# Seven block products for eight in half of a down projection, woven with the up projection, on one core

## Chip, cores, metric

The kernel runs on one core of a Trainium2 chip. The metric is the device time of one execution in microseconds (us), the median of three runs. The profile is one further execution of the same program with the hardware profiler on.

## The reference, cut to what matters

One decoder layer over 256 tokens (and 16 meta tokens) with `D_MODEL = 2048`, all float32. Two gated mixers come first; the change concerns what follows them:

```python
    h = h + rms_norm(m @ w_o[l], g_post_mix[l])
    u = rms_norm(h, g_pre_mlp[l])
    f = jnp.square(jax.nn.relu(u @ w_up[l])) @ w_down[l]     # w_up 2048 x 8192, w_down 8192 x 2048
    h = h + rms_norm(f, g_post_mlp[l])
return h[:, N_META:]
```

## The kernel before

**Split products.** Every float32 operand is kept as two parts, a high part `hi` (a rounding copy, ScalarE, line 176) and the rest `lo` (`raw - hi`, VectorE, line 179). A product is three TensorE products: hi x hi, hi x lo, lo x hi. Weights come from HBM in blocks of 1 MB (a `raw` tile, 128 x 2048 float32), loaded by the SP queue (line 173), split by `high` and `low` in `open_chunk`, and used once. There are three raw tiles and three hi/lo pairs, taken in turn, so the split of block n+2 can start only when the matmuls of block n-1 have ended. `fetch(ahead=2)` does this while block n is being used.

**The MLP** goes in `NP = 4` pieces of 2048 hidden features. In each piece the up projection comes first: `project` (called with `mm2`, lines 342 and 348) makes 128 features x 256 tokens per accumulator, weights standing in the array and tokens moving, 16 blocks of 1 MB. `evac_up` adds the two halves of an accumulator (`halves`), applies relu and square, and splits the result into `f_act`. Then the down projection: `project_t` with `block_t` (line 593) multiplies 128 tokens of `f_act` (standing) with 512 columns of `w_down` (moving); each 1 MB block takes 24 matmuls, 12 for each half of the tokens. `evac_down` adds each finished block to `F`, the sum over the four pieces. The scale of the second norm (`r2`) is applied at the end, in `times_g`.

**Order.** Each engine runs its instructions in the order in which the program issues them (`tc.manual_schedule()`); this order is written out by hand. Small work is put between matmuls by `drain` from a list `pending`.

**Ending.** The last 512 output columns are done with the second half of the tokens in two strips of 256 columns (`last_half`), so that the norm and the store of the first half run beside the last matmuls. `finish_down` multiplies by the norm factor, adds the residual and stores.

Of the kernel before, what the change touches and what calls it, by code (L numbers as in the profile page):

```python
# [11 lines left out]
ALU = mybir.AluOpType  # L12
# [4 lines left out]
CW = 512  # L17
RMS_EPS = 1e-6
LN_EPS = 1e-5


@with_exitstack
def hybrid_block(ctx: ExitStack, tc: tile.TileContext, ins: dict, out: bass.AP):
# [83 lines left out]
    NP = FF // D  # L107
    G0 = PW + 2 * CC
    HALF = (2 * CK, CW // 2)
    HALF_CW = CW // 2  # L110
# [229 lines left out]
    def mm2_high(acc, hi, act, k, cs, start, ts=slice(0, T), stop=False):  # L340
        off = act.shape[3] - T
        nc.tensor.matmul(acc.rearrange("p (a t) -> p a t", a=2)[:, :, ts], hi[:, k[0], cs],  # L342
                         act[:, k[1], :, off + ts.start:off + ts.stop], start=start, stop=stop,
                         skip_group_check=True)
# [31 lines left out]
    def halves(acc, name):  # L376

        t = tmp.tile([P, T], F32, tag="v", bufs=5, name=f"half_{name}")
        nc.scalar.copy(t, acc[:, :T])
        s = tmp.tile([P, T], F32, tag="v", bufs=5, name=f"sum_{name}")  # L380
        nc.vector.tensor_add(s, t, acc[:, T:])
        return s

    def split(dst, k, src):
        def f():
            nc.scalar.copy(dst[:, k, 0, :], src)
            nc.vector.tensor_sub(dst[:, k, 1, :], src, f32(dst[:, k, 0, :]))
        late.append(f)
# [415 lines left out]

    for n in range(NB - 1):
        project_t(m_of, KD, evac_o(n), f"o{n}")
        if n == 0:
            g_mlp = big.tile([P, D], F32, tag="c", name="g_mlp")
            nc.gpsimd.dma_start(g_mlp, ins["g_post_mlp"].broadcast_to([P, D]))
    u2 = m  # L810

    def u2_tiles(t0, n, k0, nk):
# [17 lines left out]
                f32(u2[:, k0 + i, 0, sl]), op0=ALU.mult, op1=ALU.subtract)  # L830
        return high, low


    f_act = []

    def f_of(k):
        return f_act[k // (KD // 2)][:, k % (KD // 2), :, :]

    def evac_up(j0):
        def f(j, acc):  # L840
            s = halves(acc, f"up_{j0 + j}")
            nc.vector.scalar_tensor_tensor(s, s, 0.0, s, op0=ALU.max, op1=ALU.mult)
            split(f_act[(j0 + j) // (KD // 2)], (j0 + j) % (KD // 2), s)
        return f

# [86 lines left out]
    up_high(2, 1)  # L932
    up_low(2)
    hi, lo = fetch()
    for b in range(2):
        room = big.tile([P, b * LINE + KD * T], F32R, tag=f"s{b}", name=f"f_act{b}")
        f_act.append(room[:, b * LINE:].rearrange("p (k a t) -> p k a t", k=KD // 2, a=2))
    for j, acc in enumerate(accs):
        for k in range(CK):
            kk = 3 * CK + k  # L940
            cs = slice(j * P, (j + 1) * P)
            if kk < KD - 1:
                mm2(acc, hi, lo, u2, (k, kk), cs, False, False)
            else:
                mm2_low(acc, lo, u2, (k, kk), cs)
                mm2_high(acc, hi, u2, (k, kk), cs, False, stop=True)
        flush(1)
        evac_up(0)(j, acc)
    ssq2 = const.tile([P, NT, NB], F32, name="ssq2")


    r2 = const.tile([P, NT], F32, name="r2")

    def square_h1(t, n):
        def f():
            square_of(h1[:, t, block(n)], ssq2, t, n)
        return f

    def scale2():
        nc.vector.reduce_sum(r2, ssq2, axis=mybir.AxisListType.X)  # L960
        nc.vector.tensor_scalar(r2, r2, 1.0 / D, RMS_EPS, op0=ALU.mult, op1=ALU.add)
        nc.vector.reciprocal(r2, r2)

    pending += [(1, square_h1(t, n)) for t in range(NT) for n in range(NB)]
    pending += [LATER, LATER, (1, scale2)]

    F = big.tile([P, NT, D], F32, tag="k8", bufs=2, name="F")
    ov = out[0].rearrange("(t p) d -> p t d", p=P)

    def evac_down(i, n):  # L970
        sl = block(n)

        def f(t, acc):
            if i == 0:
                nc.vector.tensor_copy(F[:, t, sl], acc)
                return
            nc.vector.tensor_add(F[:, t, sl], F[:, t, sl], acc)
            if i == NP - 1:
                square_of(F[:, t, sl], norm3.ssq, t, n, scale=r2[:, t:t + 1])
                times_g(t, sl)  # L980
                if n == NB - 2:
                    norm3.start(t)
        return f

    def times_g(t, sl):
        nc.vector.scalar_tensor_tensor(F[:, t, sl], F[:, t, sl], r2[:, t:t + 1], g_mlp[:, sl],
                                       op0=ALU.mult, op1=ALU.mult)

    def finish_down(t, cuts):

        for n, (c0, c1) in enumerate(zip(cuts, cuts[1:])):
            sl = slice(c0, c1)
            nc.vector.scalar_tensor_tensor(F[:, t, sl], F[:, t, sl], norm3.r[:, t], h1[:, t, sl],
                                           op0=ALU.mult, op1=ALU.add)
            (nc.sync, nc.scalar)[n % 2].dma_start(ov[:, t, sl], F[:, t, sl])
# [10 lines left out]
    last_f = acc_tiles("f_last", NT + 1)  # L1006
    last_ssq = const.tile([P, 2], F32, name="last_ssq")
    col_halves = [slice(h * HALF_CW, (h + 1) * HALF_CW) for h in range(2)]

    def last_half(h, kc, hi, lo):  # L1010
        cs = col_halves[h]
        block_t(last_f[1 + h][:, cs], hi[:, :, cs], lo[:, :, cs], f_of, kc, KD, 1)

    n = KD // CK - 3
    for kc in range(n):
        hi, lo = fetch()
        block_t(last_f[0], hi, lo, f_of, kc, KD, 0)
        for h in range(2):
            last_half(h, kc, hi, lo)
    three = [fetch(2 - i) for i in range(3)]  # L1020
    for i, (hi, lo) in enumerate(three):
        block_t(last_f[0], hi, lo, f_of, n + i, KD, 0)
    sl = block(NB - 1)
    nc.vector.tensor_add(F[:, 0, sl], F[:, 0, sl], last_f[0])
    square_of(F[:, 0, sl], norm3.ssq, 0, NB - 1, scale=r2[:, 0:1])
    norm3.finish(0)
    times_g(0, sl)
    finish_down(0, range(0, D + 1, CW))
    for h, cs in enumerate(col_halves):
        for i, (hi, lo) in enumerate(three):  # L1030
            last_half(h, n + i, hi, lo)
        sl = slice((NB - 1) * CW + cs.start, (NB - 1) * CW + cs.stop)
        s = tmp.tile([P, HALF_CW], F32, tag="v", bufs=5, name=f"last_{h}")
        nc.vector.tensor_add(s, F[:, 1, sl], last_f[1 + h][:, cs])
        junk = tmp.tile([P, CW], F32, tag="junk", bufs=1, name=f"sq_last_{h}")
        nc.scalar.activation(junk[:, cs], s, AF.Square, scale=r2[:, 1:2],
                             accum_out=last_ssq[:, h:h + 1])
        nc.vector.scalar_tensor_tensor(F[:, 1, sl], s, r2[:, 1:2], g_mlp[:, sl],
                                       op0=ALU.mult, op1=ALU.mult)
        if h == 0:  # L1040
            nc.vector.scalar_tensor_tensor(norm3.v[:, 1], last_ssq[:, 0:1], 1.0 / D,
                                           norm3.v[:, 1], op0=ALU.mult, op1=ALU.add)
    for f in norm3.steps(1, last_ssq[:, 1:2]):
        f()
    finish_down(1, (0, HALF_CW, CW + HALF_CW, 2 * CW + HALF_CW, D - HALF_CW, D))


# [23 lines left out]
```

## Time and profile before

| what | value |
|---|---|
| median of 3 runs | 1234.48 us (1234.24 to 1234.86) |
| the profiled execution: its own time / span of its instructions | 1235.01 us / 1233.1 us |
| TensorE busy, granted clock | 1222.1 us (99%), 0.998 |
| VectorE busy / ScalarE busy | 807.6 us (65%) / 541.6 us (44%) |
| HBM read | 234.12 MB, 192 GB/s over the span |

The page gives busy time by engine and by group of instructions; "idle before" is the time in which an engine waited just before that group, and what ended it. Because matmuls are pipelined, a matmul of 512 columns shows a duration of 389 ns while the next one starts 227 ns after it; rates are therefore read from chains of many matmuls.

### The profile page before, as it was taken

Reading aid. Unit: us, or ns where it says so; the run is one execution under the profiler, and the core shown is the slowest. Engines: PE = TensorE matmul, PEld = TensorE weight load, DVE = VectorE, ACT = ScalarE, POOL = GpSimd, SP = SyncE. Lnnn points to the kernel's source line nnn. Section 1 sums busy time; section 2 is a strip of 40 time slices with the busy share of each in tenths; the row PEclk is TensorE's granted clock in tenths of the full one; section 3 lists DMA queues with packets and bytes.
Section 4 is the critical chain, followed back from the end, with each engine's and each line's share of the span. In section 5 each row is a group of like instructions: output and inputs, shape, how many; then the busy total and the mean of one; then the engine's idle time right before and its main releaser. Section 6 shows DMA issues by size and latency. Waiting matters only on the chain.

```text
span 1233.1 us, 15685 instructions
## 1 busy us (share of the span) xinstructions
PE 1222.1 (99%) x6572; PEld 1059.6 (86%) x6572; DVE 807.6 (65%) x938; ACT 541.6 (44%) x571; POOL 6.1 (0%) x18
## 2 busy tenths in 40 slices
PE   9999999999999999999999999999999999999997
PEld 8999988888888888898888888888888888888886
DVE  5799978999676654685654456554475544556555
ACT  6633344443574443564533345433344433445432
POOL 1000000000000000000000000000000000000000
PEclk9999999999999999999999999999999999999999
DMA  8655555655548565645656656556656556566551
GB/s 258 212 187 172 171 190 187 204 188 190 195 149 316 191 212 198 204 150 193 196 181 203 190 189 201 191 187 203 190 185 205 189 187 203 179 201 202 190 186 69
DMA packets 130757, 237.22 MB, mean 192 GB/s; under 512 B 3985, under 2 KB 29905, under 8 KB 130160
## 3 DMA queue, kind: packets, MB, share of 16 engines
q1 hardware_dynamic: 128768, 229.78, 57.0%
q0 software_dynamic: 768, 4.35, 0.9%
q10 hardware_dynamic: 1152, 2.11, 0.5%
q8 instruction: 51, 0.84, 0.3%
q14 instruction: 18, 0.15, 0.0%
HBM read 234.12 MB, written 2.10 MB: 192 GB/s over the span
## 4 chain that ended last, share of the span: by engine, by line
PE 98%; DMA 1%; DVE 1%; ACT 0%; ACTq 0%; DVEq 0%; issue 0%
PE acc_dn L593 26%; PE acc_up L342 19%; PE acc_gate L593 14%; PE acc_up L348 10%; PE acc_o L593 5%; PE acc_v L337 4%; PE acc_g L337 4%; PE acc_z L337 4%; PE acc_co L593 4%; PE acc_po L593 4%; PE acc_f_last L593 2%; PE acc_o_last L593 2%; DMA x_in<-in_x_dram 1%; PE ht L818 0%; PE mt L713 0%; PE xt L284 0%
## 5 line engine op out<-in xcount | busy, mean ns | idle before, releaser
L179 DVE TENSOR_TENSOR lo<-raw,hi 128x2048 fp32r<-128x2048 f32 (+1 forms) x236 | 495.2, 2101 | 352.3 <-ACT hi L176 351.9
L176 ACT CAST hi<-raw 128x2048 fp32r<-128x2048 f32 (+1 forms) x236 | 413.7, 1757 | 556.1 <-PE acc_dn L593 190.6
L342 PE MATMUL acc_up<-m,hi 128*128 128x512 f32 (+1 forms) x1008 | 338.0, 387 | 0.0
L593 PE MATMUL acc_dn<-hi,f_act 128*128 128x512 f32 x960 | 296.4, 389 | 0.0
L348 PE MATMUL acc_up<-m,lo 128*128 128x256 f32 x992 | 272.2, 278 | 0.0
L342 PEld LDWEIGHTS acc_up<-m,hi 128*128 128x128 f32 x1008 | 186.8, 188 | 38.3
L593 PEld LDWEIGHTS acc_dn<-hi,f_act 128*128 128x128 f32 x960 | 180.2, 188 | 37.5
L593 PE MATMUL acc_dn<-lo,f_act 128*128 128x512 f32 x480 | 186.9, 389 | 0.0
L348 PEld LDWEIGHTS acc_up<-m,lo 128*128 128x128 f32 x992 | 185.7, 188 | 0.5
L593 PE MATMUL acc_gate<-hi,u 128*128 128x512 f32 x512 | 158.6, 390 | 0.0
L403 DVE SCALAR_TENSOR_TENSOR c<-a,taps,c 128x256 f32<-128x256 f32 x240 | 115.5, 484 | 6.6
L593 PEld LDWEIGHTS acc_gate<-hi,u 128*128 128x128 f32 x512 | 96.1, 188 | 20.0
L593 PEld LDWEIGHTS acc_dn<-lo,f_act 128*128 128x128 f32 x480 | 90.1, 188 | 18.5
L593 PE MATMUL acc_gate<-lo,u 128*128 128x512 f32 x256 | 99.6, 389 | 0.0
L593 PE MATMUL acc_o<-hi,m 128*128 128x512 f32 x192 | 59.6, 390 | 0.0
L593 PEld LDWEIGHTS acc_gate<-lo,u 128*128 128x128 f32 x256 | 48.1, 188 | 9.8
L337 PE MATMUL acc_v<-u,hi 128*128 128x272 f32 x256 | 49.8, 293 | 0.0
L337 PE MATMUL acc_g<-u,hi 128*128 128x272 f32 x256 | 47.5, 287 | 0.0
L337 PE MATMUL acc_z<-u,hi 128*128 128x272 f32 x256 | 47.4, 287 | 0.0
L593 PEld LDWEIGHTS acc_o<-hi,m 128*128 128x128 f32 x192 | 36.0, 188 | 7.4
L593 PE MATMUL acc_co<-hi,s_act 128*128 128x512 f32 x128 | 40.4, 392 | 0.0
L337 PEld LDWEIGHTS acc_v<-u,hi 128*128 128x128 f32 x256 | 39.8, 188 | 0.4
(222 smaller groups left out, 1061.5 us busy)
## 6 DMA issues: line engine op xcount, KB each, us to landing
raw<-in_w_up_dram SPq DMA_DIRECT2D x64, 1024.0 KB, 5.3
raw<-in_w_down_dram SPq DMA_DIRECT2D x64, 1024.0 KB, 5.1
raw<-in_w_in_dram SPq DMA_DIRECT2D x54, 1024.0 KB, 5.0
raw<-in_w_o_dram SPq DMA_DIRECT2D x16, 1024.0 KB, 5.0
raw<-in_w_pool_out_dram SPq DMA_DIRECT2D x8, 1024.0 KB, 5.2
raw<-in_w_conv_out_dram SPq DMA_DIRECT2D x8, 1024.0 KB, 5.1
raw<-in_w_in_dram SPq DMA_DIRECT2D x8, 256.0 KB, 8.0
h<-in_x_dram POOLq DMA_DIRECT2D x1, 2048.0 KB, 9.6
```

The source lines that it names most:

```text
L176: nc.scalar.copy(hi[:, sl, :], raw[:, sl, :])
L179: nc.vector.tensor_sub(lo[:, sl, :], raw[:, sl, :], f32(hi[:, sl, :]))
L337: nc.tensor.matmul(acc, w[:, k[0], cs], act[:, k[1], a, off:], start=first and n == 0, stop=last and n == 2)
L342: nc.tensor.matmul(acc.rearrange("p (a t) -> p a t", a=2)[:, :, ts], hi[:, k[0], cs], act[:, k[1], :, off + ts.start:off + ts.stop], start ...
L348: nc.tensor.matmul(acc[:, :T], lo[:, k[0], cs], act[:, k[1], 0, off:], start=False, stop=stop, skip_group_check=True)
L403: nc.vector.scalar_tensor_tensor(c, conv["a"][:, q, i:i + T], taps[:, q, i:i + 1], c, op0=ALU.mult, op1=ALU.add)
L593: nc.tensor.matmul(acc, act(kk)[:, a_, ts_], w_[:, k, :], start=kk == 0 and n == 0, stop=kk == nk - 1 and n == 2)
```

## The change

The MLP goes in eight pieces of 1024 hidden features. In each piece the down projection sees the weights as two rows (512 features each, index 1 and 2) of four column blocks of 512. Column blocks 2 and 3 are multiplied as before (products `X1` to `X4`, 24 matmuls each), but accumulate over all pieces in four PSUM banks. Column blocks 0 and 1 form a 2 x 2 block matrix B11, B12, B21, B22; with the two halves of the tokens as the other side this is a 2 x 2 by 2 x 2 block product, done in Strassen's manner (Winograd's form) as seven products `P1` to `P7` of 12 matmuls each in place of eight. For these, sums of weight blocks are made in place in the raw tile (four per piece, `SUM_FOR`), four sums and differences of the activations (`S1` to `S4`) are made and split, and each of the seven results is added from its bank to `F` (`give`).

The order of products is a written text, up products `U..` between the others (`U0b1` is the up block for feature half 0, pair b, half 1 of the inner dimension; `+` means the next piece). Everything in this part is put into a `Plan` with an engine, a cost, reads and writes; `Plan.order` is a list scheduler that keeps the given order on TensorE and SP and chooses the order on VectorE and ScalarE. Up blocks are 1024 x 256 instead of 512 x 512 (still 1 MB). The raw tiles are five (three as before, two in the place of tiles no longer needed). The factor of the second norm is now needed before the squares: `R` is two small matmuls that spread it over the partitions, and relu multiplies by it. `g_mlp` is loaded at the end on the SP queue and not early on the POOL queue. The ending keeps the two strips for the last two products.

```diff
+class Plan:
+    HOP = 0.15
+    FIXED = ("PE", "SP")
+    def add(self, engine, cost, f, reads=(), writes=(), late=0.0):
...
+    def order(self):
...
-    for i in range(NP):
-        standing_chunks.update(range(len(stream), len(stream) + NB * KD // CK))
-        for h in range(NB):
-            stream += columns(w_up, 0, KD, i * D + h * CW)
-        for n in range(NB):
-            stream += columns(w_down, i * KD, KD, n * CW)
+    PF = 2 * CW
+    NP = FF // PF
...
+    FIRST_PIECE = "U1a0 U1a1 R U1b0 U1b1 P1 X1 X3"
+    PIECE = "U1a0 U1a1 P1 X1 U1b0 U1b1 X3"
+    NEXT = "U0a0+ P5 X2 P6 X4 P7 U0a1+ P3 U0b0+ P2 U0b1+ P4"
+    LAST_PIECE = "U1a0 P1 U1a1 U1b0 U1b1 X1 P5 X2 P6 P3 P7 P2 P4 X3 X4"
...
+    SUM_FOR = {"P5": ("B11", "B12"), "P6": ("B11", "B22"), "P7": ("B12", "B22"),
+               "P4": ("B11", "B21")}
...
+            if what == "sum":
+                a_, b_ = (room_of[r][:, :CK * CW] for r in rooms)
+                plan.add("DVE", 2.29, lambda: nc.vector.tensor_add(a_, a_, b_),
+                         reads=names, writes=names[:1])
...
+                plan.add("ACT", 1.91, high, reads=names, writes=(f"hi{q}",))
+                plan.add("DVE", 2.29, low, reads=names + [f"hi{q}"], writes=(f"lo{q}",))
...
+        def relu():
+            s = box["s"]
+            nc.vector.scalar_tensor_tensor(s, s, 0.0, rb[:, None, :T].broadcast_to([P, 2, T]),
+                                           op0=ALU.max, op1=ALU.mult)
...
+    BANK = {"P1": "a", "P6": "a", "P7": "a", "P4": "a", "P5": "b", "P3": "b", "P2": "b"}
...
+    def product_block(m_, s, i):
+        h, f = FORM[s]
+        plan.add("PE", 2.72, lambda: down(banks[BANK[s]], split_at[m_], h, f, s in OPENS, True),
+                 reads=half_names(m_) + act_names(h, f), writes=(BANK[s],))
+        give(s, i)
...
+        if s == "R":
+            plan.add("PE", 0.9, rows2, reads=("diag2",), writes=("b",))
...
-    for i in range(NP):
-        for h in range(1 if i == 0 else 0, NB):
-            project(u2, KD, evac_up(h * CW // P), f"up{i}{h}", shape=(CK, CW), fill=1.0)
-        for n in range(NB):
-            if i < NP - 1 or n < NB - 1:
-                project_t(f_of, KD, evac_down(i, n), f"dn{i}{n}")
...
+    finish_down(1, (0, 384, D // 2, D // 2 + CW, D - HALF_CW, D))
+    plan.emit()
```

More of the change, by code (lines that the diff above doesn't have):

```diff
@@ L934, in hybrid_block @@
     hi, lo = fetch()
-    for b in range(2):
[L936 to L943, printed above, removed]
-            else:
[L945 to L948, printed above, removed]
+    flush()
@@ new lines, in raw_of @@
+    def raw_of(s, i):
+        return (RAW_OF.get(s, s), i)
+    uses = []
+    for m_, (s, i) in enumerate(products):
+        if m_ >= len(opened):
+            if s in SUM_FOR:
+                uses.append((m_, "sum", [(r, i) for r in SUM_FOR[s]]))
+            uses.append((m_, "split", [raw_of(s, i)]))
+    last_use = {}
+    to_load = []
+    for n, (_, _, raws_) in enumerate(uses):
+        for r in raws_:
+            if r not in last_use:
+                to_load.append(r)
+            last_use[r] = n
@@ new lines, in hybrid_block, with load, loads @@
+    free_rooms = list(room_of)
+    room_at = {}
+    def load(r):
+        src, (rows, width) = source(*r)
+        room = room_at[r] = free_rooms.pop(0)
+        plan.add("SP", 3.2, lambda: nc.sync.dma_start(
+            room_of[room].rearrange("p (k c) -> p k c", k=rows), src),
+            writes=(f"raw{room}",), late=2.0)
+    def loads():
+        while to_load and free_rooms:
+            load(to_load.pop(0))
+    split_at = {}
+    first_n = at["n"] - len(opened)
+    for m_, (hi_, lo_, _) in enumerate(opened):
+        split_at[m_] = {"hi": hi_, "lo": lo_}
@@ L965, in hybrid_block @@
[L965 to L983, printed above, removed]
@@ new lines, in hybrid_block @@
+    loads()
+    for t in range(NT):
+        for n in range(NB):
+            plan.add("ACT", 0.92, square_h1(t, n), writes=("junk", "ssq2"))
+    plan.add("DVE", 0.4, mean2, reads=("ssq2",), writes=("v2",))
+    plan.add("ACT", 0.3, root2, reads=("v2",), writes=("q2",))
+    plan.add("DVE", 1.2, diag2, reads=("q2", "v2"), writes=("diag2",))
+    unscaled = [(0, pr, 0, accs[2 * pr:2 * pr + 2], [f"x{pr}{j}" for j in range(2)])
+                for pr in range(2)]
+    m_ = 0
+    tail = len(products) - 2
@@ new lines, in sum_of_squares, with times_g @@
+    def sum_of_squares(t, n):
+        src, name = tokens_of(t, n)
+        plan.add("ACT", 0.92, lambda: square_of(src, norm3.ssq, t, n), reads=(name,),
+                 writes=("junk", f"ssq{t}{n}"))
+    def times_g(t, n):
+        src, name = tokens_of(t, n)
+        plan.add("DVE", 0.69, lambda: nc.vector.tensor_mul(
+            dst_of(t, n * CW, (n + 1) * CW), src, g_mlp[:, block(n)]),
+            reads=(name, f"raw{room_g}"), writes=(f"out{t}{n}", name if n < 2 else f"raw{room_f}"))
+    for t in range(NT):
+        for n in range(NB - 1):
+            sum_of_squares(t, n)
+            times_g(t, n)
+        plan.add("DVE", 0.4, lambda t=t: norm3.start(t),
+                 reads=[f"ssq{t}{n}" for n in range(NB - 1)], writes=(f"v{t}",))
@@ L989, in finish_down @@
+    plan.add("DVE", 0.69, lambda: nc.vector.tensor_copy(Fx[:, 1, 1, :], banks["x11"]),
+             reads=("x11",), writes=("rest", f"raw{room_f}"))
     def finish_down(t, cuts):
         for n, (c0, c1) in enumerate(zip(cuts, cuts[1:])):
[L992 to L995, printed above, removed]
@@ L1027, in hybrid_block @@
[L1027 to L1042, printed above, removed]
@@ new lines, in hybrid_block @@
+    ends = [(m_, "X3"), (m_ + 1, "X4")]
+    for w, s in ends:
+        h = AT[s][0]
+        plan.add("PE", 2.72, lambda w=w, h=h: down(banks["x10"], split_at[w], h, A1, False, h == 1),
+                 reads=half_names(w) + act_names(h, A1), writes=("x10",))
+    sum_of_squares(0, NB - 1)
+    times_g(0, NB - 1)
+    plan.add("DVE", 1.5, lambda: norm3.finish(0), reads=("v0", f"ssq0{NB - 1}"), writes=("r0",))
+    finish_down(0, range(0, D + 1, CW))
+    col_halves = [slice(h * HALF_CW, (h + 1) * HALF_CW) for h in range(2)]
```

378 lines of the change are left out of this document (335 added, 43 removed).

## Prediction

> **What bounds the kernel now.** I read the page first, then the chain of waits in order of time, the table by windows, the groups with shapes kept apart, and stretches of the timeline. Page: busy time, and the chain by engine.
>
> ```profile
> PE 1222.1 (99%) x6572; PEld 1059.6 (86%) x6572; DVE 807.6 (65%) x938; ACT 541.6 (44%) x571; POOL 6.1 (0%) x18
> ...
> PE 98%; DMA 1%; DVE 1%; ACT 0%; ACTq 0%; DVEq 0%; issue 0%
> ```
>
> TensorE never waits; only less matmul work, or a wait put in, can move the time. The chain in order of time (start, us, what) gives its rate:
>
> ```profile
> 614.30 87.10 PE acc_dn L593 x384
> ...
> 1136.70 65.30 PE acc_dn L593 x288
> 1202.00 22.42 PE acc_f_last L593 x144
> ```
>
> 87.10 / 384 = 226.8 ns for a matmul of 512 columns, so 12 take 2.72 us and a 24-matmul block 5.44. An up block also takes 5.44 (87.06 us from 875.52 to 962.58, 16 blocks). What the splits cost, and what they wait for (groups, shapes apart):
>
> ```profile
> L179 DVE TENSOR_TENSOR lo<-raw,hi 128x2048 fp32r<-128x2048 f32 x212 | 485.7, 2291 | 351.7 <-ACT hi L176 351.4
> L176 ACT CAST hi<-raw 128x2048 fp32r<-128x2048 f32 x212 | 404.8, 1910 | 555.7 <-PE acc_dn L593 190.6 <-PE acc_up L342 136.5 <-PE acc_gate L593 71.5
> ```
>
> Low waits for high, high waits for TensorE to release a pair: today the splits have slack. By windows (the third "busy (x)" column is VectorE), a gate stage and an up stage:
>
> ```profile
> 234.00:308.00 74.00, 74.00 (x328) 61.02 (x326) 71.04 (x98) 29.37 (x21) 0.00 (x0) 1.00 0.57 190
> ...
> 702.00:790.00 88.00, 88.00 (x517) 77.74 (x517) 52.64 (x61) 39.99 (x47) 0.00 (x0) 1.00 0.61 195
> ```
>
> The gate stage shows VectorE 96% busy (71.04 of 74) with TensorE gapless at full clock: a full VectorE does not itself slow TensorE.
>
> **Matmuls removed.** Eight pieces each lose 12 matmuls: 96 x 226.8 ns = 21.8 us. The strips of 256 columns halve in number: the last 144 matmuls took 22.42 us where the rate gives 48 x 0.2268 + 96 x 0.1134 = 21.8, so half of 0.65 goes: 0.3. Together **-22.1**.
>
> **VectorE per piece, against TensorE.** TensorE: 12 blocks x 5.44 + 7 x 2.72 = 84.3 us. VectorE: 19 lows x 2.29 = 43.5; four weight sums; 7 gives x 0.69 (F<-F,acc_dn: 683 ns) = 4.8; 8 totals x 0.42 = 3.3; 4 relus x 0.75 = 3.0 (three-operand 512-wide rows: 746 to 751); 8 form sums x 0.42 = 3.4; 8 form lows x 0.69 = 5.5. No row shows a weight sum: 512-wide adds (0.69) give 2.8 for 2048 columns, 1024-wide (1.22) give 2.4, the low (same size, two float32 inputs) 2.29; I take 2.29, so 9.2. Sum 72.7 of 84.3 (86%), against 48.8 of 87 for the same features now (stages at 614 and 702: 45.0 + 52.6 for 2048 features). ScalarE, 19 x 1.91 plus about 12, is far from full. The mean fits; the question is the order.
>
> **Steady pieces.** With three pairs, the split of product n+2 starts when n-1 ends. The timeline shows the lag:
>
> ```profile
> 1191.16 1.91 ACT L176 CAST hi<-raw 128x2048 fp32r<-128x2048 f32 x1 [3.53 <-PE acc_dn L593]
> ...
> 1193.10 2.29 DVE L179 TENSOR_TENSOR lo<-raw,hi 128x2048 fp32r<-128x2048 f32 x1 [3.15 <-ACT hi L176]
> ```
>
> The block of acc_f_last starts at 1201.84, so the block boundary is 1201.84 - 2 x 5.44 = 1190.95: high starts 0.2 after it, low 1.94 later, ready 4.4 us after the boundary. The window, a P plus a block, is 8.16. I walked the emitted order of one middle piece with these durations, time 0 at U1a0. The tight stretch runs from P5's sum to P4's low: 50 us of VectorE work while TensorE needs 54 from X3 to P4. Ready against due: S1's low 39.2 / 40.8 (P5); low part of A, pair b, 42.1 / 43.5 (X2); S2's low 48.6 / 49.0 (P6); P3's low 63.5 / 65.3; the total that frees the second up bank 70.3 / 70.7. Nothing is late, but three margins are about 0.4. Raw rooms: B21 can load only when P7's split frees its tile (53.6), lands 59.0 and is summed at once. Its price from the DMA rows (KB each, us to landing):
>
> ```profile
> raw<-in_w_down_dram SPq DMA_DIRECT2D x64, 1024.0 KB, 5.1
> ...
> raw<-in_w_in_dram SPq DMA_DIRECT2D x8, 256.0 KB, 8.0
> ...
> g_mix<-in_g_post_mix_dram POOLq DMA_DIRECT2D x1, 1024.0 KB, 12.1
> ```
>
> I take 5.1 (same load); 8.0 would delay P3 by 1.1. For missed margins I book 0.25 per piece, 7 pieces: **+1.7** (from 0 to 2 each).
>
> **First piece.** The relu needs rb, so ScalarE's eight squares (0.73 each), which now hide under 60 us of up blocks, come early. ScalarE: second up block's high ends 546.4 (its load issued at 539.25, 5.3 to land), seven squares to 551.5, high 553.4, square 554.1, two halves, a high to 556.7, root 556.9. VectorE then: low to 559.05, Newton steps and diagonals to 560.6. R is queued on TensorE behind U1a1, which ends at 557.8 (541.5 + 3 x 5.44), so all later matmuls wait from 557.8 to 560.7. R takes 0.5 (six such matmuls in 0.96 now), and U1b0 must wait for both relu-scale and the totals in VectorE's queue: 563.2 instead of 557.8, +5.4. X3 then waits for its activations' low part: 582.9 against 582.2, +0.7. **+6.1** (from 4 to 9).
>
> **Last piece.** No up blocks of a next piece cover the P's. By the same walk: P1 +0.5 (low part of A); P5 waits for S1 (relu, square, S1, its high and low behind lows of X1, P5, X2 and a sum): ready 33.0 where X1 ends 30.5, +2.5; P7, P2, P4 a tenth each. **+3.3** (from 1 to 8).
>
> **Tail.** Before, TensorE ended 8.65 us before the span did. Now VectorE, fully queued, still has two gives, nine 512-wide products and copies, and the first half's norm and stores ahead of the last strip: last strip's add 69.4 where TensorE ends 66.2; last F 74.9; the store's landing and end 3.4 as now: 12.1 us after TensorE. **+3.5** (from 0 to 6). g_mlp's load goes to SP, behind X4's raw: 51.4 + 12 at worst against its use at 58.9; I book nothing, at worst 4.5.
>
> **Sum.** Span 1233.1 - 22.1 + 1.7 + 6.1 + 3.3 + 3.5 = 1225.6. The profiled execution lies 1.9 above its span, the median 0.5 below that: +1.4 gives **1227.0**.
>
> **Clock after a wait.** A row that speaks against waits: the same kind of transposes at the start and in mid-kernel,
>
> ```profile
> 4.75 2.10 PE L270 MATMUL idle<-ident 128*128 128x128 f32 x10
> ```
>
> is 0.21 each, while ht at 519.14 ran four in 0.44, 0.11 each. Coming from rest TensorE ran at half rate; from 2.69 to 6.85 at least. If a wait in the middle brings this back, 4.2 us at half rate cost 2.1, once (R) or twice (P5). [...]
>
> **Rivals.**
> 1. *VectorE's queue runs late once in every steady piece* (slower). Place: X3 to P4. Its in-order queue stands behind a sum whose block has not landed, or a low behind a give; P6, P3 or the next up block wait. For: margins of 0.4, 92% load there. Against: before, lows at 96% load in the gate stage stayed gapless, and loads land in 5.1. Price 7 x lateness: at 0.7 to 1.6 us per piece no change (1232 to 1237), above 1.6 slower; at 2.2 per piece, 1241.
> 2. *The clock halves after the waits*: 1227.0 + 2.1 to 4.2 = 1229 to 1231.
> 3. *The waits at the ends are mostly absent*: ends at half of 12.9, steady at nothing: 1219; all gone, 1212.4 (1233.1 - 22.1 + 1.4). Against: ScalarE's squares ahead of R are in its queue whatever happens.
>
> **Chances.** This kernel's measurement can tell about 0.2% (2.5 us): faster is below 1232.0, slower above 1237.0. Forecast (1222 to 1232) 0.42; rival 2, 0.12; rival 3, 0.06; rival 1 in its middle 0.18, beyond 0.22. So faster 0.60, same 0.18, slower 0.22. Range 1221 to 1240: it leaves out about 0.05 below and 0.14 above. The likeliest case's own range is 1222 to 1232.
>
> **What would show it.** In the chain: pieces of about 84.3 us; one wait near 558 of about 5 us ending in a VectorE total; one of 2 to 3 before P5 of the last piece, ended by a form's low; TensorE ending about 12 us before the span's end; VectorE at 86% between. Weight sums near 2.29. I am wrong if pieces take over 86 us, with TensorE waiting for lo, a form or a raw block; or if matmuls after the wait start 0.45 us apart.

## The result and the profile after

| | before | after |
|---|---|---|
| median, runs side by side | 1234.67 us (1234.24 to 1235.16, 4 runs) | 1220.37 us (1219.27 to 1221.35, 4 runs) |
| the profiled execution: time / span | 1235.01 / 1233.1 us | 1221.17 / 1219.4 us |

The ratio is 0.9884, with a 95% interval from 0.9867 to 0.9901: 14.3 us off, where 7.5 were forecast. The page of the changed kernel, busy time and the chain by engine:

```profile
PE 1202.4 (99%) x6456; PEld 1040.0 (85%) x6456; DVE 977.3 (80%) x1059; ACT 625.4 (51%) x644; POOL 5.6 (0%) x17
...
PE 96%; DVE 2%; DMA 1%; ACT 1%; issue 0%; ACTq 0%; DVEq 0%
```

VectorE has gone from 65% to 80%, and TensorE is still the chain. The waits of TensorE from 530 us on (who waited for whom: us in total, times, longest):

```profile
PE bank_u L418 <- DVE F_raw L1175: 2.0, 1, 2.0
PE bank_b L1255 <- DVE forms L1226: 1.4, 1, 1.4
```

So there are two waits in the whole MLP, one in the first piece and one in the last (the view lists waits over 0.15 us). A steady piece by windows, from one first up product `U1a0` to the next (PE, PEld, VectorE, ScalarE, POOL, clock, DMA share, GB/s):

```profile
636.16:720.72 84.56, 84.56 (x438) 72.33 (x437) 69.00 (x59) 46.03 (x41) 0.00 (x0) 1.00 0.62 198
...
560.61:564.33 3.72, 3.72 (x13) 3.19 (x13) 3.72 (x5) 2.68 (x6) 0.00 (x0) 0.55 0.17 60
```

All six steady pieces last 84.56 us with no wait of TensorE; VectorE has 69.0 to 69.7 of it. The last row lies behind the first wait: there the granted clock is 0.55 on average. The profiler's record of the granted clock has exactly 0.5 from 560.97 to 564.38 us, 3413 ns; this is called the half clock below. The timeline shows how that wait came about (start, duration, engine, what; in brackets the idle time before and what ended it):

```profile
541.71 1.91 ACT L252 CAST hi<-raw 128x2048 fp32r<-128x2048 f32 x1 [1.41 <-DMA raw<-in_w_up_dram]
...
557.91 0.68 PE L1155 MATMUL bank_b<-diag,ones 128*128 128x128 f32 x4
557.93 1.90 ACT L1112 CAST hi<-raw_m 128x2048 fp32r<-128x2048 f32 x1 [3.06 <-PE bank_u L418]
...
559.74 0.64 ACT L1168 COPY half<-bank_u 128x256 f32<-128x256 f32 x2
...
560.61 0.51 PE L418 MATMUL bank_u<-m,hi 128*128 128x512 f32 x1 [2.02 <-DVE F_raw L1175]
...
561.13 0.63 PE L418 MATMUL bank_u<-m,hi 128*128 128x512 f32 x1
...
561.77 0.63 PE L418 MATMUL bank_u<-m,hi 128*128 128x512 f32 x1
```

The first row, the high part of the second up block, is for the account of the prediction below. `R` ran at 557.91 without a wait. `U1b0` then waited 2.02 us for the totals that free the up banks; those waited for two half copies on ScalarE, and the copies stood behind the high part for `P1`, which only became ready at 557.93. From 561.13 on a pair of matmuls (512 and 256 columns) starts every 0.64 us; at full clock it is 0.34.

The wait of `P5` in the last piece:

```profile
1172.86 2.29 DVE L1100 TENSOR_TENSOR raw_c<-raw_c,raw_m 128x2048 f32<-128x2048 f32 x1
...
1175.06 0.68 DVE L1226 TENSOR_TENSOR forms<-F_raw,forms 128x512 fp32r<-128x512 f32 x1
...
1175.80 0.73 PE L1255 MATMUL bank_b<-hi,forms 128*128 128x512 f32 x2 [1.42 <-DVE forms L1226]
```

ScalarE made S1's high part from 1172.97 to 1173.59, but VectorE had begun the weight sum for `P6` 0.1 us before that; S1's low part came 1.5 us after its high.

The end, where the last matmul starts at 1208.49 and the last strip's addition comes 1.9 us after that matmul has ended:

```profile
1208.49 0.28 PE L1255 MATMUL bank_u<-hi,forms 128*128 128x256 f32 x1
...
1210.64 0.41 DVE L1427 TENSOR_TENSOR last<-raw_a,bank_u 128x256 f32<-128x256 f32 x1
```

**Where the time went.** From the span of before, 1233.1 us, in us:

| part | forecast | measured | read from |
|---|---|---|---|
| matmuls | -22.1 | -22.1 | by count and rate: 96 fewer at 0.2268, strips halved |
| pace of the first up stage | not in it | -1.7 | next paragraph |
| first piece | +6.1 | +4.4 | 557.9 to 560.61 (2.7), half clock (1.7) |
| steady pieces | +1.7 | +1.7 | 84.56 against 84.32, seven times |
| last piece | +3.3 | +2.3 | `U1a0` at 1143.52 to the last matmul's end: 65.2 against 62.9 |
| tail | +3.5 | +1.95 | 10.62 from TensorE's end to the span's end, 8.67 before |
| start | 0 | -0.28 | the fourth up block begins at 541.06, before at 541.34 |

They add to 1219.4, as measured; the forecast's add to 1225.6.

**The pace.** In the kernel before the up matmuls of the MLP's first stage go slower than those of later ones. The chain of before, a first stage and a later one:

```profile
553.75 0.23 PE acc_up L342
554.45 0.23 PE acc_up L342
...
889.13 0.23 PE acc_up L342
891.85 0.23 PE acc_up L342
```

From 553.75 to 554.45 there are two pairs in 0.70 us, 0.350 each; from 889.13 to 891.85 eight in 2.72, 0.340 each; the granted clock is 1.00 in both. In before the slow pace (0.2333 us per 512 columns, against 0.2267) lasts from 541 to about 616, just behind the change from the up products to the first down product at 614.1; in after it ends with the first wait, at 558. The 59 us between are 1.7 us at 2.9%.

### The profile page after: what moved, and what is told of

It reads as the page before. It is cut to its first block, busy times and chain, and to the rows that moved or that the text cites. A ratio compares the mean times of both kernels' runs of the same rounds, so it can differ in the third digit from the quotient of the medians.

```text
span 1219.4 us, 15714 instructions
## 1 busy us (share of the span) xinstructions
PE 1202.4 (99%) x6456; PEld 1040.0 (85%) x6456; DVE 977.3 (80%) x1059; ACT 625.4 (51%) x644; POOL 5.6 (0%) x17
## 4 chain that ended last, share of the span: by engine, by line
PE 96%; DVE 2%; DMA 1%; ACT 1%; issue 0%; ACTq 0%; DVEq 0%
PE bank_u L418 18%; PE acc_gate L669 14%; PE acc_up L1255 13%; PE bank_u L424 9%; PE bank_a L1255 7%; PE bank_b L1255 5%; PE acc_o L669 5%; PE acc_v L413 4%; PE acc_z L413 4%; PE acc_g L413 4%; PE acc_co L669 4%; PE acc_po L669 4%; PE acc_o_last L669 2%; PE acc_up L418 1%; DMA x_in<-in_x_dram 1%; PE acc_up L424 1%
## 5 line engine op out<-in xcount | busy, mean ns | idle before, releaser
L418 PE MATMUL bank_u<-m,hi 128*128 128x512 f32 x960 | 331.2, 391 | 2.0 <-DVE F_raw L1175 2.0
L252 ACT CAST hi<-raw 128x2048 fp32r<-128x2048 f32 (+1 forms) x114 | 180.8, 1594 | 228.0 <-PE acc_gate L669 71.5
L255 DVE TENSOR_TENSOR lo<-raw,hi 128x2048 fp32r<-128x2048 f32 (+1 forms) x114 | 215.4, 1895 | 75.5 <-ACT hi L252 75.1
L424 PE MATMUL bank_u<-m,lo 128*128 128x256 f32 x960 | 266.2, 277 | 0.0
L1117 DVE TENSOR_TENSOR lo<-raw_m,hi 128x2048 fp32r<-128x2048 f32 x87 | 199.0, 2289 | 52.2 <-ACT hi L1112 51.9
L1112 ACT CAST hi<-raw_m 128x2048 fp32r<-128x2048 f32 x87 | 166.3, 1912 | 140.2 <-PE bank_u L418 75.3
L418 PEld LDWEIGHTS bank_u<-m,hi 128*128 128x128 f32 x960 | 181.0, 189 | 40.3 <-DVE F_raw L1175 2.2
L424 PEld LDWEIGHTS bank_u<-m,lo 128*128 128x128 f32 x960 | 181.0, 189 | 1.6
L1255 PE MATMUL acc_up<-hi,forms 128*128 128x512 f32 x496 | 157.6, 389 | 0.0
L1255 PE MATMUL acc_up<-lo,forms 128*128 128x512 f32 x248 | 96.6, 389 | 0.0
L1255 PE MATMUL bank_a<-hi,forms 128*128 128x512 f32 x256 | 84.3, 390 | 0.0
```

The lines of the kernel that those rows point to most:

```text
L252: nc.scalar.copy(hi[:, sl, :], raw[:, sl, :])
L255: nc.vector.tensor_sub(lo[:, sl, :], raw[:, sl, :], f32(hi[:, sl, :]))
L1112: nc.scalar.copy(box["flat"], raw)
L1117: nc.vector.tensor_sub(lo, raw, f32(box["flat"]))
L1255: nc.tensor.matmul(acc, forms[h][:, f, k, a_, :], box[w_][:, k, cs], start=start and k == 0 and n == 0, stop=stop and k == KH - 1 and n == ...
```

## The experiments

The first four ran on one chip, the other eight on another; each was timed beside the kernel before. Where an edit is compared with the changed kernel, this is its median of 1220.37 from other rounds (with e11 and e12, that of their own rounds). The kernel before itself differed by 2 us from rounds to rounds, so what is said of differences of 1 to 2 us rests on the profiles and not on the medians. "The e2 version" is the kernel of the second.

**e1: cover for the gap behind R.** Eight matmuls of 512 columns that nobody reads, behind `R`:

```diff
             nc.tensor.matmul(banks["b"][:, t * P:(t + 1) * P], ones, box2["diag"][t],
                              start=True, stop=True)
+        for _ in range(8):
+            nc.tensor.matmul(banks["a"].rearrange("p (a t) -> p a t", a=2), u2[:, 0, 0, 0:P],
+                             u2[:, 0, :, :], start=True, stop=True, skip_group_check=True)
```

> Edit: eight matmuls of 512 columns, whose result nobody reads, fill the time between R and U1b0 in the first piece (8 x 0.227 = 1.8 us against an idle gap of about 2.0 us). Theory (the gap itself halves TensorE's clock afterwards, in the executions in which it falls badly): U1b0 still starts near 560.6, but runs at the full rate, the granted clock after it reads 1.00, and the time is 1219.3 to 1219.6 us in all executions, where the changed kernel has 1219.3 to 1219.6 in some and 1221.2 to 1221.4 in others. Rival (the half rate has another cause, R's small float32 matmuls or something that comes round by itself): the stretch after U1b0's start still shows a clock near 0.55 in some executions, and the two groups of times remain.

Measured: 1219.83 us (1219.69 to 1221.30; before 1234.67), span 1218.2. The profiled execution has no half clock in the MLP, and `U1b0` starts at 560.73, as in after. But the slow pace (0.2356 per 512 columns here) went on to about 572 and did not end at 558 as in after: 11.5 us at 3.9% give back 0.4. So in the profiled pair the gap makes the half clock; filling it gains 0.5 us in the median, which these runs can't tell from none. One of the four executions still took 1221.30; it wasn't profiled, and what made it 1.6 us slower is not known.

**e2: half copies ahead of P1's high.** One dependence more, in the first piece:

```diff
-                plan.add("ACT", 1.91, high, reads=names, writes=(f"hi{q}",))
+                after_halves = ["t0", "t1"] if products[m_] == ("P1", 0) else []
+                plan.add("ACT", 1.91, high, reads=names + after_halves, writes=(f"hi{q}",))
```

> Edit: in the first piece the high part of P1's weights is ordered on ScalarE behind the two half copies of U1a, which it stood ahead of while it waited for TensorE. Theory (U1b0 waits for the first bank because the half copy is queued behind that high part): U1b0 starts within 0.7 us of R's end instead of 2.0, TensorE keeps its clock, and the time falls to 1217.5 to 1218.2 us, 1.5 below the changed kernel's quick executions and 3.2 below its others. Rival (ScalarE and VectorE are simply full there): the high part of P1, 0.7 us later, makes P1 or X1 wait, and the time stays at 1219 to 1221.

Measured: 1218.24 us (1217.59 to 1220.36), ratio to before 0.9869 (0.9854 to 0.9884). The slowest of the four, 2.1 us over the next, was not profiled and stays unexplained. The timeline of the fastest:

```profile
558.69 0.50 PE L418 MATMUL bank_u<-m,hi 128*128 128x512 f32 x1 [0.41 <-DVE F_raw L1176]
```

ScalarE now does both copies first, and the high at 558.08. The wait falls from 2.02 to 0.41 us, there is no half clock, and the slow pace still ends there (0.2267 from 560 on). What ScalarE does first at 557.9 makes the wait of the first piece; `R` and its chain do not.

**e3: the last piece with more products ahead of P5.**

```diff
-    LAST_PIECE = "U1a0 P1 U1a1 U1b0 U1b1 X1 P5 X2 P6 P3 P7 P2 P4 X3 X4"
+    LAST_PIECE = "U1a0 U1a1 U1b0 U1b1 P1 X1 P5 X2 P6 P3 P7 P2 P4 X3 X4"
```

> Edit: in the last piece P1 goes from behind U1a0 to behind U1b1, so that P1 and X1 lie between U1b1 and P5. Theory (P5 waits for S1's low part, 2.1 us, and TensorE's end follows): the wait before P5 is under 0.3 us and the last matmul ends about 2 us earlier. Then two answers on the time: if TensorE sets the end, it falls by about 2 (to 1217.3 to 1219.3); if VectorE's queue from the splits of X3 and X4 on sets the end, by less than 1, since that queue holds 20 us of work without a gap.

Measured: 1222.91 us (1222.07 to 1223.57), 2.5 over the changed kernel. `P5` waited longer, not less:

```profile
1186.28 0.73 PE L1255 MATMUL bank_b<-hi,forms 128*128 128x512 f32 x2 [2.01 <-DVE forms L1226]
```

VectorE was full from 1171 on, and S1's low (1185.54) stood behind another split (1183.34, 2.28 us). The half clock follows this wait, from 1187.54. More matmuls ahead brought more splits into VectorE's queue ahead of S1; the wait is one of VectorE's order, not of too little cover.

**e4: P4's matmuls twice in every piece** (its product counts double in the output):

```diff
-        plan.add("PE", 2.72, lambda: down(banks[BANK[s]], split_at[m_], h, f, s in OPENS, True),
-                 reads=half_names(m_) + act_names(h, f), writes=(BANK[s],))
+        def matmuls():
+            for again in range(2 if s == "P4" else 1):
+                down(banks[BANK[s]], split_at[m_], h, f, s in OPENS, True)
+        plan.add("PE", 2.72, matmuls, reads=half_names(m_) + act_names(h, f), writes=(BANK[s],))
```

> Edit: the 12 matmuls of P4 are done twice in each of the eight pieces (its product counts double in the output); the order on all engines is unchanged. Theory (TensorE sets the pace of the steady pieces, so the eighth product that was saved was worth its full price): 8 x 2.72 = +21.8 us, a steady piece goes from 84.56 to 87.2, time 1241 to 1243. Rival (VectorE's queue sets the pace and TensorE has hidden slack): a piece grows by less than 1.5 us, time under 1232.

Measured: 1241.32 us (1240.12 to 1242.35), 20.9 over the changed kernel; 96 matmuls at the rate are 21.8. A steady piece, from one `U1a0` to the next (637.24 to 724.52), takes 87.3 us, 2.7 more than 84.56, as forecast. The matmuls that the change takes out are worth their full time: the steady pieces are TensorE's.

**e5: VectorE's low of P6 twice.**

```diff
-                    nc.vector.tensor_sub(lo, raw, f32(box["flat"]))
+                    for again in range(2 if products[m_][0] == "P6" else 1):
+                        nc.vector.tensor_sub(lo, raw, f32(box["flat"]))
```

> VectorE splits off the low part of P6's weights twice in every piece (the second time gives the same result): 2.3 us more of VectorE per piece, put where P6 must be ready soonest after P5; its share of a steady piece goes from 69.0 to about 71.3 of 84.56 us. If VectorE really has the slack that its 82% say (the theory that the steady pieces are bounded by TensorE alone, as the prediction said), the six steady pieces stay within 0.5 us of 84.56 and the whole comes out 0 to 3 us over the changed kernel: 1220 to 1223. If VectorE is the near bound through its order (the prediction's first rival, which had it late by a few tenths at margins of 0.4), P6 is 2 us late in each piece, seven pieces give 14 to 16 us, and the time is 1234 to 1237.

Measured: 1231.50 us (1229.22 to 1233.50, 10 runs; before 1232.60). Between the two expectations. `P5` starts at 676.5, 762.4 and 848.3 in successive pieces, so a piece by windows is:

```profile
676.50:762.43 85.93, 84.89 (x438) 72.33 (x437) 71.22 (x60) 46.13 (x41) 0.00 (x0) 1.00 0.61 196
```

VectorE has 2.2 us more and the piece is 1.37 longer, with TensorE waiting once per piece (PE busy 84.89 of 85.93) though VectorE still has 14.7 us idle in it. The wait is that of `P6` for the low part of S2, which VectorE makes behind the doubled operation. Both theories missed: the 15 us are no slack, and the order of VectorE has about 0.85 us of it at this place. In the last piece a further wait came in:

```profile
PE bank_a L1256 <- ACT hi L1112: 2.0, 1, 2.0
```

**e10: half of that low twice**, to see whether the margin is one:

```diff
                     nc.vector.tensor_sub(lo, raw, f32(box["flat"]))
+                    if products[m_][0] == "P6":
+                        half = slice(0, CK * CW // 2)
+                        nc.vector.tensor_sub(lo[:, half], raw[:, half], f32(box["flat"][:, half]))
```

> VectorE splits off half of the low part of P6's weights twice in every piece: about 1.1 us more of VectorE per piece at the place where 2.29 us more made each piece 1.37 us longer. If the order of VectorE has a fixed margin there, 2.29 - 1.37 = 0.9 us, a steady piece takes 84.56 + 1.1 - 0.9 = 84.8 us, between 84.7 and 84.9, and the six 1 to 2 us more in all. If the cost is in proportion (0.6 of what is added), it takes 85.2 us.

Measured: 1223.09 us (two runs, 1221.95 and 1224.23). The addition costs 1.22 us, and a piece is

```profile
674.70:759.54 84.84, 84.84 (x438) 72.26 (x437) 70.26 (x60) 46.12 (x41) 0.00 (x0) 1.00 0.61 199
...
560.11:563.50 3.39, 3.39 (x19) 3.00 (x20) 3.39 (x4) 2.68 (x6) 0.00 (x0) 1.00 0.18 66
```

0.28 longer: 1.25 more of VectorE less a margin of 0.97. The loss lies where it lay in e5: three matmuls of `P6` (683.15, 683.51, 683.85) start 0.36 and 0.34 apart where 0.23 is usual. A fixed margin it is, 0.85 to 0.97 us in each piece, and not a cost in proportion. (The second row is for the clock, below.)

**e6: the kernel before, with a pause of TensorE.**

```diff
                 mm2_high(acc, hi, u2, (k, kk), cs, False, stop=True)
+        if j == 3:
+            gap = const.tile([P, 32], F32, name="gap")
+            nc.vector.tensor_copy(gap, acc[:, :32])
+            nc.tensor.matmul(misc_tile("spot")[:, :32], ones, gap, start=True, stop=True)
         flush(1)
```

> The kernel before, with a pause of TensorE put in after the first up block of the MLP: VectorE copies 32 columns of the fourth accumulator, and a 32 wide matmul that nobody reads waits for the copy. In the kernel before a 512 wide matmul there takes 0.2333 us from about 541 until 617 us and 0.2267 afterwards; in the changed kernel the slow pace ends at its wait at 558 us. If a pause of TensorE ends the slow pace, matmuls go at 0.2267 from about 550 us on: 2.8% of some 65 us, 1.8 us off, less the pause of 0.7 to 2: the first down block starts 0 to 1.2 us sooner than before and the whole takes 1233.4 to 1234.7 (1.7 us more if the clock halves for 3.4 us behind the pause). If the pace belongs to the work of this stretch (its loads, its mixture of shapes), it stays at 0.2333 until 617 and the whole takes 1235.2 to 1236.7.

Measured: 1234.55 us against 1232.60 for before beside it, ratio 1.0019 (1.0010 to 1.0029). Both kernels give two values: this one six executions at 1234.1 to 1234.6 and four at 1236.3 to 1236.9, before 17 at 1232.2 to 1233.0 and two at 1234.2 and 1234.5. The profiled execution, of the faster kind, has 0.2264 to 0.2270 from 550 us on. The pause took 1.2 us of waiting and cost 1.7 to 2.2, and the slower kind is there in spite of it: if that kind is the slow pace, a pause doesn't end it as a rule. That the pause ended it in the profiled execution isn't shown either: e5, e7, e10, e11 and e12 have the fast pace from 549 on without any pause there. The 2 us between the kinds are what 76 us at 2.8% give; that the slower kind is the slow pace, here and in before, follows from this size alone, since only the faster kind of this kernel and only the slower of before have a profile.

**e7: less of VectorE in the tail** (on the e2 version):

```diff
-        plan.add("DVE", 0.69, lambda: nc.vector.tensor_mul(
+        engine, eng = ("POOL", nc.gpsimd) if n < 2 else ("DVE", nc.vector)
+        plan.add(engine, 0.69, lambda: eng.tensor_mul(
             dst_of(t, n * CW, (n + 1) * CW), src, g_mlp[:, block(n)]),
...
-    plan.add("DVE", 0.69, lambda: nc.vector.tensor_copy(Fx[:, 1, 1, :], banks["x11"]),
+    plan.add("ACT", 0.64, lambda: nc.scalar.copy(Fx[:, 1, 1, :], banks["x11"]),
```

> On top of the version with the half copies ahead of P1's high (1218.24): in the tail the four products of the finished columns 0 and 1 with g_mlp go from VectorE to GpSimd, and the copy of the rest from VectorE to ScalarE, 3.0 us of VectorE out of its queue between 1196 and 1206. If VectorE's gapless queue sets the tail (there 1204.7 to 1215.8, 11.1 us, against 8.65 in the kernel before), the last strips' additions come right behind their matmuls and the tail falls to 9 to 9.5 us: 1216.0 to 1217.0. If the tail is set by the last additions' own chain or GpSimd is too slow or disturbs VectorE, it stays at 10.7 or more: 1218 to 1220.

Measured: 1219.66 us (before 1232.60, ratio 0.9893, 0.9878 to 0.9907); the tail is 11.05 us, against 10.61 in the e2 version. VectorE now has holes, 1.89 us before 1201.72 and 0.72 before 1202.79, each ended by a square on ScalarE, where the moved copy stands; GpSimd takes 5.06 us for its four products. Counted from TensorE's end, the finish of the first tokens starts 0.4 us later than in the e2 version (1204.73 with the end at 1206.35, against 1203.21 and 1205.20). Taking work from VectorE moved the limit to ScalarE's squares.

**e8: the weight sum of P6 in the last piece on GpSimd** (on the e2 version):

```diff
-                plan.add("DVE", 2.29, lambda: nc.vector.tensor_add(a_, a_, b_),
+                on_pool = products[m_] == ("P6", NP - 1)
+                plan.add("POOL" if on_pool else "DVE", 4.5 if on_pool else 2.29,
+                         lambda eng=nc.gpsimd if on_pool else nc.vector: eng.tensor_add(a_, a_, b_),
```

> On top of the version with the half copies ahead of P1's high (1218.24): in the last piece the sum of the raw weights for P6 goes from VectorE to GpSimd. In that version the sum runs on VectorE from 1169.28 to 1171.56, ahead of S1's low at 1171.48 that P5 waits 1.4 us for. If the sum's place in VectorE's queue makes P5's wait, P5 starts without one and the whole takes 1216.5 to 1217.5 (GpSimd's sum may take 4 to 5 us and P6 isn't due before 1177). If S1's chain is late for itself, or GpSimd's sum comes too late for P6, the time stays at 1218 or rises to 1220.

Measured: 1222.24 us (before 1232.60): slower, for a reason that neither theory had. Its timeline:

```profile
1165.75 4.65 POOL L1102 TENSOR_TENSOR raw_c<-raw_c,raw_m 128x2048 f32<-128x2048 f32 x1 [778.09 <-ACT half L1171]
...
1166.16 4.79 DVE L1186 SCALAR_TENSOR_TENSOR F_raw<-F_raw,rb 128x512 f32<-128x512 f32 x1
```

GpSimd took 4.65 us, in time for `P6`. But VectorE's relu, 0.69 us elsewhere, took 4.79: it started 0.41 after GpSimd's sum and ended 0.55 after it. S1's chain comes after that relu, and `P5` waited 3.46 us instead of 1.42; a half clock followed from 1174.48. The sum's place in VectorE's queue was not tested by this.

**e11: S1's low ahead of that sum** (on the e2 version), a dependence instead:

```diff
+                behind = ["S1l"] if products[m_] == ("P6", NP - 1) else []
...
-                         reads=names, writes=names[:1])
+                         reads=names + behind, writes=names[:1])
```

> On top of the version with the half copies ahead of P1's high: in the last piece VectorE's sum of the raw weights for P6 stays behind the low part of S1. If that sum's place in VectorE's queue makes P5's wait of 1.4 us, the wait is under 0.3 us and the whole 1.4 to 2.1 us under the version without it: 2.5 to 4 us under the changed kernel in the same rounds. If it only moves the wait to P6 or P3, the gain over the changed kernel stays at 1 to 2 us.

Measured: 1217.99 us (1217.84 to 1218.42), where the changed kernel beside it has 1221.01 and before 1234.53; ratio to before 0.9865 (0.9849 to 0.9881). Its waits of TensorE:

```profile
PE bank_a L1257 <- DVE F_raw L1279: 1.0, 1, 1.0
PE bank_u L418 <- DVE F_raw L1177: 0.4, 1, 0.4
PE bank_b L1257 <- DVE forms L1228: 0.2, 1, 0.2
```

`P5`'s wait has shrunk from 1.4 to 0.2, but 1.0 has come back at 1185.65, where a product waits for VectorE to empty bank a. The sum's place made `P5`'s wait; VectorE is so full there that most of it turns up again. Most of the 3.0 us under the changed kernel is what e2 had already (2.1), and a gain over e2 isn't shown: the medians differ by 0.25, and in the profiles the last matmul ends at 1205.44 here and at 1205.20 in e2.

**e12: the first strip ahead of the first tokens' finish** (on top of the last):

```diff
-    finish_down(0, range(0, D + 1, CW))
...
+        if e == 0:
+            finish_down(0, range(0, D + 1, CW), behind=("v1",))
```

> The version with S1 first, and in the tail VectorE does the first half strip of the last product before it finishes the first 128 tokens. If VectorE's order sets the tail, the second strip's addition, 1.2 us later than it needs to be, comes about 1 us sooner and the tail falls from 10.6 to 9.6 us: 3.5 to 5 us under the changed kernel in the same rounds, the fastest of all. If the tail hangs on the outputs' DMAs of the first tokens, which now leave later, it gains nothing or loses up to 1 us against S1 first alone.

Measured: 1217.94 us (1217.65 to 1218.27), the fastest, but 0.05 under S1 first alone, which is nothing. VectorE does the first strip's addition at 1203.27 instead of 1206.12, but the second strip's still starts 1.68 us after TensorE's end (1.88 in e11), and the tail is 10.5 us instead of 10.6: the queue is full, and an exchange within it gains next to nothing. This version is 3.1 us under the changed kernel and 16.6 under before (ratio 0.9864, 0.9849 to 0.9880).

**e9: the changed kernel again**, in the rounds of the last ones:

> The changed kernel itself, on the chip and in the rounds of the three runs beside it, to see which of its terms are the kernel's and which the execution's. The theory that the half clock of 3.4 us and the slow pace of 0.2333 are states of an execution: its times again fall into groups about 1.7 to 2 us apart, and the kernel before in the same rounds too (1232.6 and 1234.5 were seen). The rival, that both belong to the kernels: one value each within 0.3 us, at a ratio of 0.9884.

Measured: 1221.01 us (1220.22 to 1221.49, 4 runs), before 1234.53 (1234.49 to 1235.28), ratio 0.9889 (0.9871 to 0.9906). The four values lie within 1.3 us: neither two groups 1.7 to 2 apart nor one value within 0.3. The profile repeats: waits of 2.0 and 1.4, half clock for 3.41 us, slow pace to 558. Before, on the chip where it took 1232.6 in 17 of 19 executions with e5 to e8, took 1234.5 to 1235.3 now in all six. So its 2 us don't belong to the chip. By subtraction, the changed kernel would gain nearer 12 us against the faster kind; the two were not timed side by side.

## Why the prediction was right and wrong

The direction came as forecast, and so did what carries it. The median of 1220.37 lies 6.6 us under the forecast of 1227.0 and 0.6 us under the stated range. Of the steps that failed, two are the largest with 1.7 us each: the wait of `R` in the first piece, which wasn't there, and the pace of the first up stage, which was put at nothing.

- **Matmuls, right.** -22.1, and e4 shows 20.9 for as many put back. It carries the direction.
- **First piece: the place right, the reason wrong.** The step that failed reads "second up block's high ends 546.4 (its load issued at 539.25, 5.3 to land)". That high ended at 543.6 (541.71 and 1.91); its load is the one issued at 535.8, in before at 536.05, and I had taken the second of the two blocks loaded ahead for the first. All of ScalarE's queue and VectorE's low, Newton steps and diagonals were put 2.5 to 2.9 us too late with it, and `R` was given a wait of 2.9 that it did not have (in e1 and e4, whose profiles have it, it is 0.5 and 0.4). The "one wait near 558 of about 5 us ending in a VectorE total" was 2.0, ended by such a total, but the late one was the half copy behind `P1`'s high (e2). X3's +0.7 did not come.
- **The clock, rival 2: it came.** Priced at 2.1 per wait from rest, it measured 1.7, half of 3.41 us. (The 4.2 us at half rate were read too long: the transposes at the start follow each other 0.21 apart until 6.30 and 0.11 from 6.46 on.) The record of the granted clock has 0.5 for 3413 ns, from 560.97 on. That followed a wait of 2.02 us, and one of 1.87 in e5; behind `P5`'s 1.42 the clock stayed at 1.00.
- **Steady pieces: the size right by chance.** The 0.25 per piece stood for missed margins, and there were none. TensorE never waits in 84.56 us; the 0.24 more than in my 84.3 lies in its own rate, 0.2273 per 512 columns in this mixture of products (84.56 over the worth of 372) against 0.2267 in before. The weight sums, for which no row of before had a price, take the 2.29 that was assumed. Rival 1 (VectorE late once in every piece) did not happen, but its mechanism is real: the margin of S2's low ahead of `P6`, which I put at 0.4, turned out at 0.85 to 0.97, and 1.25 us of VectorE more brought 0.28 per piece. VectorE's 69.0 to 69.7 against my 72.7 fits that: an operation behind another one starts about 0.08 us sooner than the durations say (two lows in a row begin 2.2 apart).
- **Last piece, a little too dear.** `P5` "+2.5" measured 2.1, wait and restart; P1's +0.5 was none.
- **Tail, mechanism right, size off.** The last strip's addition was to come 3.2 us after TensorE's end and came 1.9 after; the tail was 10.6 and not 12.1. e7 and e12 show that neither work taken from VectorE's queue nor an exchange in it shortens it; what would is open.
- **The pace: a term that I did not have.** 1.7 of the 6.2 us between forecast and span. The rows of before held it (13 blocks of the first stage take 72.8 us, and 13 x 5.44 is 70.8); I took the rate from later stages for all. What sets it is open: e6 has a slower kind, 2 us apart, in four of ten executions in spite of its pause; in the profiled e7, e11 and e12 the fast pace of 549 turned slow at `U1b0`'s 0.4 us wait; and in e3, whose edit changes the order of the last piece only, a slow pace went on through a wait of 2.1 us there.

Of the 6.2 us, then: pace 1.7, first piece 1.7 (no wait at `R` and none at X3, less the half clock), tail 1.55, last piece 1.0, start 0.3. Rival 3, the end waits mostly absent at 1219, was nearest in time, but by the table its terms stood at 8.65 of 12.9 and not at half, and the pace brought the time near it: that is luck.

## What to carry to other kernels

Fewer matmuls are worth their full time (e4: 20.9 us of 21.8) as long as the engines that feed them keep their margin at the tightest place (0.85 to 0.97 us a piece here); read that margin by adding work just there, since the idle share of the engine (18% here) says nothing on it. Where a chain with deadlines shares an in-order engine with long splits, look at what the scheduler puts just ahead of each deadline: one dependence on a half copy gave 2.1 us in the median and a reordered last piece cost 2.5. And take a rate from the very stage in which it will be used.

## What the runs showed of the hardware

**The half clock follows a grid.** In after the record of the granted clock has its first full clock at 4.60 us and half clock from 560.97 and from 1212.92, 163 and 354 times 3413.3 ns later; in before it has the first full clock at 6.41 and half clock from 1228.38, 358 times later. In e9 the half clock of the end starts at 1212.45, and 191 times 3413.3 ns ahead of it lies 560.50, from where to 563.9 a pair of matmuls takes 0.64 us instead of 0.34. Cut the time into windows of 3413.3 ns counted from the first full clock or from the start of a half clock (560.50 in e9, 560.43 in e5, 1187.54 in e3, 1174.48 in e8; behind the last matmul 1208.32 in e2, 1232.18 in e4, 1214.12 in e10; that these runs keep the same grid is taken from after, before and e9), and lay TensorE's waits over them (the ends of matmuls are modelled, so a wait is good to about 0.1 us):

| run | TensorE idle, ended at | by window | clock after |
|---|---|---|---|
| e8 | 3.46, 1174.19 | 0.33 and 3.13 | half |
| after / e9 | 2.02, 560.61 / 2.03, 560.24 | all in one | half |
| e3 | 2.01, 1186.28 | all in one | half |
| e5 | 1.87, 560.27 | all in one | half |
| e5, last piece | 2.02, 1199.02 | 1.72 and 0.29 | full |
| e10 | 1.87, 560.11 | 0.52 and 1.35 | full |
| e2, P5 | 1.42, 1172.22 | all in one | full |
| after, P5 | 1.42, 1175.80 | 0.99 and 0.43 | full |
| e4 | 1.57, 560.76 | 0.57 and 1.00 | full |
| e3, first piece | 2.08, 560.48 | 1.10 and 0.98 | full |

Behind a gap of 1.87 us within one window the next one had the half clock (e5); behind one of the same length across a border it had not (e10), nor behind one of 2.08 (e3). By this table the most idle time of a window that full clock followed is 1.72 us, and the least that the half clock followed is 1.87. The latter hangs on the windows of after, e5 and e9, which also hold `R`'s four small matmuls; without those it is 2.01. The unprofiled executions can't be laid over the grid. The four of the changed kernel lie at 1219.3, 1219.6, 1221.2 and 1221.4, about 1.7 us apart, which fits one kind with the half clock and one without; only the third is known to have it.

**VectorE beside GpSimd.** In e8 a relu with both inputs in SBUF took 4.79 us beside GpSimd's sum of 4.65, where the 32 of the changed kernel take 0.68 to 0.70. In e7 three products of VectorE with one input in PSUM ran beside GpSimd, which worked from 1198.07 to 1203.13:

```profile
1197.74 1.28 DVE L1385 TENSOR_TENSOR raw_a<-acc_up,raw_m 128x512 f32<-128x512 f32 x2
...
1198.07 5.06 POOL L1385 TENSOR_TENSOR F_raw<-F_raw,raw_m 128x512 f32<-128x512 f32 x4 [809.81 <-ACT ng_offset=None)_0_0_9194 L860]
...
1202.79 0.69 DVE L1385 TENSOR_TENSOR raw_a<-acc_up,raw_m 128x512 f32<-128x512 f32 x1 [0.72 <-ACT ng_offset=None)_3_0_9265 L860]
```

They took their usual time: 1.28 us for two in a row and 0.69 for one, where one of the changed kernel takes 0.68. Whether the place of the inputs makes the difference is not shown: the relu and the products differ in more than that, and so do GpSimd's two jobs.

**Several paces at granted clock 1.00.** From 549 us on, in the first up stage, the profiled runs have 0.2356 us per 512 columns (e1, e2, e3, e8), 0.2333 (before, after, e4, e9) or 0.2267 (e5, e7, e10, e11, e12), up to 3.9% apart, and the record of the clock doesn't show it: in before it has 1.00 at 0.2333 (553.75 to 554.45) and at 0.2267 (889.13 to 891.85). The pace changes at some interruptions of TensorE and not at others: behind the first piece's wait it is 0.2267 in after, e2 and e4, 0.2333 in e3, e7, e11 and e12, and still 0.2356 in e1 and e8. Where it was slow then, it became 0.2267 within 3 us of the first product that followed the up products (614.1 in before, 570 to 572 in the others), and stayed there. Why is open.
